# Attention scores q·kᵀ: input loads issued behind a head's third copy instead of its second

## The chip, the cores and the metric

The kernel runs on one core of a Trainium2 chip. The time is device time in microseconds (us) for one launch. The runs before the change gave a median of 1063.17 us (three runs, 1063.16 to 1063.77).

The core's engines have short names here: PE does matmuls (PEld is its weight loads), DVE, ACT and POOL are the vector, scalar and general engines, SP issues transfers. Each has its own queue of instructions, which it works through in order. A transfer (DMA) is issued by an instruction on SP's or ACT's queue and then carried out by 16 DMA engines, which all transfers share.

## The reference

```python
def setup_inputs():
    batch, n_heads, seq, head_dim = 8, 12, 1024, 64
    # q, k: (8, 12, 1024, 64) float32, normal, times 0.1

def reference(q, k):
    return np.einsum('bhid,bhjd->bhij', q, k).astype(np.float32)
```

For each of 96 heads (8 x 12), a 1024 x 64 matrix q is multiplied with the transpose of a 1024 x 64 matrix k. The inputs are 50.3 MB together, the result is 402.7 MB: a head's result alone is 4 MB.

## The kernel before

**Blocks.** The 96 heads are cut into 11 blocks of 2, 2, 4, 8, 8 and then six times 12 heads (line 33), numbered 0 to 10 here. A block's q and k are each loaded with one transfer (`Block.load`, line 66; the DMA is line 73), except in blocks 0 and 1, which are loaded head by head (line 84). A load of a 12-head block is 3072 KB, of an 8-head block 2048 KB. Blocks 0 to 2 are loaded at once into a tile that is later used for results ("early"). The others go into tiles of a pool with two places (`in_pool`, tag "x", the tile is `x_sb`), so a load has to wait until the content of two loads before has been cast.

**From load to matmul.** POOL casts a loaded tile to 16 bit in pieces (line 127, `cast_quads`), into a pool of five `half_sb` tiles. DVE transposes each piece in 32 x 32 squares (line 145, `transpose_quads`) into the block's `qT` and `kT`, of which there are two sets: one for the block being computed, one for the next. Blocks 0 and 1 go another way, through PE (line 151).

**A head.** `scores` (line 156) computes one head. With w = 2, which holds for all but the first head, it runs four steps, u = 0 to 3. In each, PE does four matmuls into one of two PSUM tiles `ps` (line 171), and ACT copies that tile, 128 x 2048 numbers, into the head's result tile `o_sb` (line 181). There are three result tiles. After a step, `scores` calls whatever the dictionary `side` holds for that u. Behind the fourth copy, SP issues the head's result as one transfer of 4096 KB (line 185). A head can only begin to copy when the result of three heads before has been written out.

**Where the next loads are issued.** `block` (line 238) calls `scores` for each head of a block and fills `side`: under 0 the transposes for the next block, and, in two heads of each block, under 1 a call of `next_load`, which takes the next (block, q or k) from the list `stream` and issues its load on ACT's queue. Which heads these are stands in `LOADS` (line 263): heads 1 and 3 of block 2, heads 4 and 6 of blocks 3 and 4, heads 6 and 8 of the later ones. What is loaded during block i belongs to block i + 2. The first two loads into `x_sb`, block 3's, are issued before all heads (line 217), one on SP's queue and one on ACT's.

**Order.** Every instruction is given to `keep_in_program_order` (`pin`), so each engine's queue runs in the order in which the code is written. After a head, `to_half` (line 225) puts the casts of what has been given a load by then into POOL's queue, up to block i + 2.

Of the kernel before, what the change touches and what calls it, by code (L numbers as in the profile page):

```python
# [13 lines left out]
def kernel(  # L14
# [6 lines left out]
    nc = tc.nc  # L21
# [190 lines left out]
    def next_load(eng):  # L212
        if stream:
            b, x = stream.pop(0)
            b.load(x, eng)
# [9 lines left out]
    def to_half(last):  # L225
        while casts:
            i, c = casts[0]
            if i > last or (blocks[i], c[0]) in stream:
                return
            blocks[i].cast_quads(*c)  # L230
            casts.pop(0)
# [6 lines left out]
    def block(i, heads, ps_pool, w):  # L238
        b = blocks[i]
        nxt = blocks[i + 1] if i + 1 < len(blocks) else None  # L240
        for n in heads:
            side = {}
            if nxt and nxt.by_pe:
                if n == 1:
                    side = {
                        u: [
                            lambda x=u // 2: nxt.transpose_rows(
                                x, ps_pool, nc.vector.tensor_copy
                            )
                        ]  # L250
                        for u in (1, 3)
                    }
            elif nxt:
                parts = nxt.chunks()
                some = [s for m, s in enumerate(parts) if m * b.N // len(parts) == n]
                side = {0: [lambda s=s: nxt.transpose_quads(*s) for s in some]}

            if n in LOADS.get(i, (6, 8)):
                side[1] = side.get(1, []) + [lambda: next_load(nc.scalar)]
            b.scores(n, side, ps_pool, w)  # L260
            to_half(i + 2 + (n == b.N - 1))

# [4 lines left out]
    with tc.tile_pool(name="first_pool", bufs=4, space=bass.MemoryType.PSUM) as pool:  # L267
        for x in range(2):
            blocks[0].transpose_rows(x, pool, (nc.vector.tensor_copy, nc.scalar.copy)[x])
        block(0, [0], pool, 1)  # L270
    po_pool = ctx.enter_context(
        tc.tile_pool(name="po_pool", bufs=2, space=bass.MemoryType.PSUM)
    )
    block(0, [1], po_pool, 2)
    for i in range(1, len(blocks)):
        if i + 1 < len(blocks):
            blocks[i + 1].alloc()
        block(i, range(blocks[i].N), po_pool, 2)
# [30 lines left out]
```

## Time and profile before

| what | value |
|---|---|
| median of the runs | 1063.17 us |
| profiled execution, span | 1061.2 us |
| PE busy | 701.0 us (66%) |
| ACT busy | 697.3 us (66%) |
| DVE busy | 471.3 us (44%) |
| POOL busy | 368.3 us (35%) |
| moved by DMA | 453.25 MB, mean 427 GB/s |
| result transfers | 96 of 4096 KB, median 21.8 us from issue to landing |
| loads of 12-head blocks | 12 of 3072 KB, median 22.2 us (q) and 21.9 us (k) |

The profile is of one execution; its span is the time from its first to its last instruction, and the runs' time is taken around it. A group of instructions is named by line, engine and operation, with the tile it writes and the tile it reads (`o_sb<-ps`). "Idle" is time in which the engine stood still just before that group, and behind the arrow stands what ended most of it. ACTq and SPq are the queues of ACT and SP at work, issuing a transfer for example. The DMA share is the mean busy share of the 16 DMA engines.

ACT's idle time and PE's hang together: PE waits for ACT to empty a PSUM tile (325.5 us in total, 188 times), and ACT waits for a result tile to be written out.

### The profile page before, as it was taken

The numbers are of one execution on the slowest core, as the hardware profiler recorded it, in microseconds if no ns is written. First come the engines' busy times: TensorE is split into PE (matmuls) and PEld (weight loads), VectorE is DVE, ScalarE is ACT, GpSimd is POOL, SyncE is SP. The second block draws the span as 40 slices with busy tenths as digits, with TensorE's granted clock in tenths as the row PEclk, the third lists the DMA queues.
The fourth block names the chain that finished last, engine by engine and source line by source line (L and its number), as shares of the span: only waits on it lengthen the run. The fifth ranks groups of instructions, "written<-read, shape, count | busy, mean of one in ns | idle before, by whom it ended". The sixth has DMA issues, their size and how long they took to land.

```text
span 1061.2 us, 4282 instructions
## 1 busy us (share of the span) xinstructions
PE 701.0 (66%) x1568; PEld 241.5 (23%) x1568; DVE 471.3 (44%) x75; ACT 697.3 (66%) x386; POOL 368.3 (35%) x286
## 2 busy tenths in 40 slices
PE   6866755765677557775577855777557777778770
PEld 2322211221222112221122211222112222222220
DVE  2999502990795007960079600795007950000000
ACT  4866755755677556775577755777557777777771
POOL 6967228607720463304633046320463200000000
DMA  9999999999999999999999999999999999999997
GB/s 375 434 435 434 434 432 429 432 430 429 429 434 431 429 438 429 435 422 428 434 434 433 425 424 437 432 431 426 432 430 434 434 434 430 430 435 430 433 431 319
DMA packets 17588, 453.25 MB, mean 427 GB/s; under 512 B 1952, under 2 KB 1952, under 8 KB 2976
## 3 DMA queue, kind: packets, MB, share of 16 engines
q1 hardware_dynamic: 14688, 406.85, 89.2%
q10 hardware_dynamic: 2880, 46.14, 10.3%
q8 instruction: 12, 0.20, 0.1%
q14 instruction: 8, 0.07, 0.0%
HBM read 50.33 MB, written 402.65 MB: 427 GB/s over the span
## 4 chain that ended last, share of the span: by engine, by line
DMA 71%; ACT 18%; PE 8%; issue 1%; DVE 0%; POOL 0%; ACTq 0%; SPq 0%
DMA out_dram<-o_sb 71%; ACT o_sb L181 18%; PE ps L171 8%; DMA early<-in_q_dram 0%; PE ps L151 0%; POOL half_sb L97 0%; ACTq L181 0%; DVE kT L154 0%; DVE o_sb L179 0%; ACT kT L154 0%; SPq L84 0%
## 5 line engine op out<-in xcount | busy, mean ns | idle before, releaser
L181 ACT COPY o_sb<-ps 128x2048 f32<-128x2048 f32 (+1 forms) x384 | 695.0, 1860 | 334.6 <-DMA out_dram<-o_sb 306.2
L171 PE MATMUL ps<-kT,qT 64*128 64x512 f16 x1536 | 696.9, 617 | 329.2 <-ACT o_sb L181 325.5
L127 POOL CAST half_sb<-x_sb 32x1536 f16<-32x1536 f32 (+1 forms) x256 | 346.5, 1353 | 454.5 <-DMA x_sb<-in_q_dram 315.0
L171 PEld LDWEIGHTS <-qT 64*128 64x128 f16 x1536 | 238.3, 157 | 786.0 <-issue 781.3
L145 DVE STREAM_TRANSPOSE qT<-half_sb 128x1536 f16<-128x1536 f16 (+1 forms) x34 | 232.7, 7140 | 372.0 <-issue 314.9
L145 DVE STREAM_TRANSPOSE kT<-half_sb 128x1536 f16<-128x1536 f16 (+1 forms) x34 | 234.3, 7198 | 0.0
L127 POOL CAST half_sb<-early 32x1024 f16<-32x1024 f32 x16 | 16.5, 1034 | 3.9 <-DMA early<-in_q_dram 3.2
L151 PE MATMUL ps<-ident,half_sb 128*128 128x128 f16 x32 | 4.1, 308 | 6.6 <-POOL half_sb L97 6.0
L154 DVE COPY qT<-ps 128x1024 f16<-128x1024 f16 x2 | 2.5, 1225 | 12.1 <-PE ps L151 12.1
L179 DVE COPY o_sb<-ps 128x1024 f32<-128x1024 f32 x4 | 4.9, 1224 | 4.3 <-PE ps L171 4.3
L97 POOL CAST half_sb<-early 128x512 f16<-128x512 f32 x8 | 4.6, 613 | 4.1 <-DMA early<-in_q_dram 4.1
L151 PEld LDWEIGHTS <-half_sb 128*128 128x128 f16 x32 | 3.2, 139 | 8.4 <-POOL half_sb L97 6.3
L154 ACT ACT_TABLE_LOAD x1 | 1.3, 1283 | 5.6 <-DMA early<-in_q_dram 5.6
L154 DVE COPY kT<-ps 128x1024 f16<-128x1024 f16 x1 | 1.2, 1225 | 4.3 <-PE ps L151 4.3
L154 ACT COPY kT<-ps 128x1024 f16<-128x1024 f16 x1 | 1.0, 1012 | 1.2 <-PE ps L151 1.2
masks.py:199 POOL TENSOR_SCALAR_AFFINE_SELECT ident<-ident 128x128 f16<-128x128 f16 x1 | 0.3, 292 | 0.1
masks.py:197 POOL MEMSET ident<- 128x128 f16 x1 | 0.2, 204 | 0.3 <-POOLq L293 0.3
L293 POOL MEMSET const-float32-0.0<- 128x1 f32 x1 | 0.1, 98 | 0.2 <-issue 0.2
L293 POOL MEMSET const-bfloat16-1.0<- 128x1 bf16 x1 | 0.1, 100 | 0.0
L293 POOL MEMSET const-uint8-127<- 128x1 uint8 x1 | 0.1, 100 | 0.0
L293 POOL MEMSET const-float32-1.0<- 128x1 f32 x1 | 0.1, 98 | 0.0
## 6 DMA issues: line engine op xcount, KB each, us to landing
out_dram<-o_sb SPq DMA_DIRECT2D x96, 4096.0 KB, 21.8
x_sb<-in_q_dram ACTq DMA_DIRECT2D x6, 3072.0 KB, 22.2
x_sb<-in_k_dram ACTq DMA_DIRECT2D x6, 3072.0 KB, 21.9
x_sb<-in_k_dram ACTq DMA_DIRECT2D x2, 2048.0 KB, 19.0
x_sb<-in_q_dram SPq DMA_DIRECT2D x1, 2048.0 KB, 18.2
x_sb<-in_q_dram ACTq DMA_DIRECT2D x1, 2048.0 KB, 18.5
early<-in_k_dram ACTq DMA_DIRECT2D x4, 256.0 KB, 5.0
early<-in_q_dram SPq DMA_DIRECT2D x4, 256.0 KB, 4.7
```

The source lines that it names most:

```text
L97: nc.gpsimd.tensor_copy(out=self.rows[x][:, :, half], in_=self.raw[x][:, half * n : (half + 1) * n].rearrange("p (r d) -> p r d", d=D),)
L127: nc.gpsimd.tensor_copy(out=half_sb[q0 : q0 + 32].rearrange("p (r d) -> p r d", d=32), in_=raw[32 * b : 32 * b + 32, c * m : (c + 1) * m, h],)
L145: pin(nc.vector.transpose(out=dst, in_=src))
L151: pin(nc.tensor.transpose(t_ps[:, t], self.rows[x][:, t], ident))
L154: pin(copy(out=dst, in_=src))
L171: nc.tensor.matmul(ps[:, at : at + 512], qT[cs, g, w * u + tt], kT[cs, g, js],)
L179: pin(nc.vector.tensor_copy(out=dst, in_=ps))
L181: pin(nc.scalar.copy(out=dst, in_=ps))
L293: nc = _bacc.Bacc("TRN2", target_bir_lowering=False, num_devices=1)
```

## The change

One line of `block`: the call of `next_load` goes into `side` under 2 instead of 1, so it is made behind the third of a head's four steps.

```diff
             if n in LOADS.get(i, (6, 8)):
-                side[1] = side.get(1, []) + [lambda: next_load(nc.scalar)]
+                side[2] = side.get(2, []) + [lambda: next_load(nc.scalar)]
             b.scores(n, side, ps_pool, w)
```

On ACT's queue each of these 14 loads changes places with one copy (line 181). The queues of SP, PE, DVE and POOL hold the same instructions in the same order as before, and the order in which transfers are issued is the same.

## The prediction

> **What bounds the kernel now.** I read the page's slices and queues first, then the chain of work that ended last, then the waits, and last the stretches in which a load runs beside the results.
>
> ```profile
> DMA  9999999999999999999999999999999999999997
> q1 hardware_dynamic: 14688, 406.85, 89.2%
> q10 hardware_dynamic: 2880, 46.14, 10.3%
> DMA 71%; ACT 18%; PE 8%; issue 1%; DVE 0%; POOL 0%; ACTq 0%; SPq 0%
> L181 ACT COPY o_sb<-ps 128x2048 f32<-128x2048 f32 (+1 forms) x384 | 695.0, 1860 | 334.6 <-DMA out_dram<-o_sb 306.2
> ```
>
> The two queues that carry data (q1, with nearly all its bytes from SP, and q10, with ACT's loads) keep the 16 DMA engines busy for 89.2 + 10.3 = 99.5% of the span. That is 1055.9 of 1061.2 us. The chain is mostly result transfers. ACT, the busiest compute engine beside PE, sits idle for 334.6 us, 306.2 of them until a result has landed and freed an output tile. So compute waits for the DMA engines. To be sure that this holds where the edit acts, I cut the span into stages (the columns after the length are busy time of each engine, the clock, the DMA share and GB/s):
>
> ```profile
> 0.00:20.00 20.00, 11.53 (x38) 5.12 (x39) 6.12 (x5) 6.82 (x7) 11.75 (x21) 1.00 0.94 376
> 20.00:60.00 40.00, 35.80 (x91) 12.83 (x90) 33.14 (x9) 34.09 (x20) 38.00 (x37) 1.00 1.01 425
> 60.00:200.00 140.00, 86.86 (x192) 29.69 (x192) 82.96 (x17) 86.88 (x49) 79.13 (x65) 1.00 1.00 432
> 200.00:840.00 640.00, 420.35 (x927) 143.92 (x926) 325.09 (x43) 420.94 (x233) 239.45 (x164) 1.00 1.00 431
> ```
>
> From 20 us on the DMA share is 1.00 (1.01 comes from packets counted at a stage's edge). The loads that the edit moves are issued at 56.1 us (the first) to 759.9 us (the last), all inside these stages.
>
> Now one such load, and a stretch without one (ACT's timeline; start, length, what, and in brackets the idle time before it):
>
> ```profile
> 469.28 1.86 ACT L181 COPY o_sb<-ps 128x2048 f32<-128x2048 f32 x1 [2.34 <-DMA out_dram<-o_sb]
> 469.33 0.33 ACTq L73 DMA_DIRECT2D x_sb<-in_q_dram  x1
> 471.04 1.87 ACT L181 COPY o_sb<-ps 128x2048 f32<-128x2048 f32 x1
> 473.09 3.64 ACT L181 COPY o_sb<-ps 128x2048 f32<-128x2048 f32 x2 [0.18 <-PE ps L171]
> 483.52 3.64 ACT L181 COPY o_sb<-ps 128x2048 f32<-128x2048 f32 x2 [6.79 <-DMA out_dram<-o_sb]
> ...
> 522.88 3.63 ACT L181 COPY o_sb<-ps 128x2048 f32<-128x2048 f32 x2 [5.09 <-DMA out_dram<-o_sb]
> ...
> 933.48 3.63 ACT L181 COPY o_sb<-ps 128x2048 f32<-128x2048 f32 x2 [2.32 <-DMA out_dram<-o_sb]
> ...
> 943.25 3.63 ACT L181 COPY o_sb<-ps 128x2048 f32<-128x2048 f32 x2 [2.33 <-DMA out_dram<-o_sb]
> ```
>
> The load sits behind the head's second copy in the code, yet its issue stands at 469.33, 0.05 us into the first copy: ACT's queue hands its copies on and runs ahead as long as the next one's data are there. Without loads a head takes 943.25 - 933.48 = 9.77 us. The four heads from 469.28 to 522.88, with a q and a k load among them, take 53.60 us, so the two loads cost 53.60 - 4 x 9.77 = 14.52 us. Their 2 x 3072 KB are 6.29 MB, and at the 432 GB/s of the table's third row that makes 14.56 us. A load costs its bytes, and no more.
>
> **The change, part by part.** Nothing is added or removed. 14 load issues on ACT (those in the head loop; the first two stand before it) move behind one more copy. The order of SP's, PE's, DVE's and POOL's work and the order of the DMAs among themselves stay.
>
> *The issue.* The third copy is handed on when PE has filled its tile, at 473.09 in the rows above. The load's issue should then stand at about 473.1 to 473.2 instead of 469.33: 3.8 us later (only 2 us in the head at 54 us, where the copies already wait for PE). What it now delays on ACT is the fourth copy, which lies behind the third: 1.8 us of copying cover the 0.33 us of issuing. Were this cover gone, 14 x 0.33 = 4.7 us of ACT work would be exposed. But ACT waits 2.3 us or more before each head for a landed result, so it would shorten that wait. Value taken: 0.
>
> *The wait before the issue.* A load waits until POOL has cast the input tile's previous content. The four semaphore waits recorded on the load's line took 0.017 us each. Later too there is room: block 6's k load, issued at 250.93, takes the tile of block 5's k, whose last cast ended at 201.61 + 5.97 = 207.6. A later issue only widens that gap. Cost 0, and no new wait stands before the fourth copy.
>
> *The DMA engines.* What I must exclude is that they run dry for want of the load. When ACT starts a head, the result of three heads ago has just landed and the two between are still to be written: 2 x 9.77 = 19.5 us of work. The head's own result is issued 7.5 us later (copies from 469.28 to 476.73). So 12 us of work are left at the worst moment, without any load. A load that comes 3.8 us later fits in three times. In the head at 54 us the third result before landed at 66.2, where ACT's idle time ends, so the queue is as full there. Idle time added: 0.
>
> *Who waits for the load.* POOL casts it, DVE transposes the casts, and the next block's matmuls read them. The tightest place is block 5:
>
> ```profile
> 208.82 31.16 DVE L145 STREAM_TRANSPOSE kT<-half_sb 128x1536 f16<-128x1536 f16 x4
> 271.32 1.86 PE L171 MATMUL ps<-kT,qT 64*128 64x512 f16 x4 [0.19 <-ACT o_sb L181]
> ```
>
> Its last transpose ends at 240.0 and its first matmul starts at 271.32: 31.3 us to spare, against a load that lands some 4 us later. Block 4's ends at 102.33 + 18.88 = 121.2 for a start at 178.34. From block 6 on, DVE waits 70 us and more for the transposed tiles to come free. Cost 0.
>
> *Mixing reads and writes.* This is the one cost that the trace can't exclude. Today a load starts where one result has just landed; then it will start 3.8 us into the next one's 9.77. The stretches with a pair of loads (469.3 to 522.9, 601.2 to 655.0, 733.1 to 786.7) show 426, 426 and 427 GB/s, those without (877 to 931, 931 to 985) 431 and 433. A loss of 432 - 426 = 6 over 432, times 53.7 us and 7 pairs, makes 5.2 us in the whole run, though the head starts above show none. Bounds: -5.2 us if the shift removed the loss, +5.2 if it doubled it. I take 0: the same packets meet the same number of others, shifted by 40% of a result. As the head starts see no loss at all, I keep a third of the bounds (1.7 us) for the likely case.
>
> [...] The trace first: loads take a median of 22.2 and 21.9 us from issue to landing, while their bytes are worth 7.3 us of all engines. [...]
>
> *Sum.* 1061.2 us of span + 0 for the issue, 0 for the waits, 0 for the engines, 0 for the mixing = 1061.2. The median of the runs, 1063.17, lies 2.0 us above the span, which the edit doesn't touch. Forecast 1063.2.
>
> **The rivals.** *A, faster: the loss from mixing goes.* Up to 5.2 us, so 1058.0 to 1061.0. For it: the 426 against 432 GB/s. Against it: the head starts, which charge a pair of loads no more than its bytes.
>
> *B, slower: the load meets the results at a worse phase.* Place: the two or three results written while a load is under way, 7 times a pair. Price: the loss of 5.2 us doubled, 1068.4; it decides by over 0.2% once these stretches fall from 426 to below 423.5 GB/s (2.1 us / (7 x 53.7 us) = 0.56%). For it: the q load's own stretch, 469.3 to 496.0, shows 419 GB/s and the k load's, 496.0 to 523.0, shows 433, so the place of a load in time may matter. Against it: such short stretches count packets at their edges.
>
> *C, slower: the load comes too late for block 5.* It needs 31.3 us of delay before PE waits, and then 12 more before the DMA engines do; 10 us beyond that would give 1073. The delay is 3.8 us, so I give it next to nothing.
>
> *D, the change hardly does what it says:* ACT's queue runs so far ahead that the issue moves by less than 1 us. Against it: the third copy's tile isn't filled before 473.09. It would give 1063.2 too.
>
> **How the numbers follow.** About 0.2%, 2.1 us, is what a measurement of this kernel can tell from no change. Forecast with D: 0.87 (D 0.03 of it), from 1062.0 to 1065.0, which is the third of the mixing bounds either way, a little less below since the head starts leave nothing to win. A: 0.05. B: 0.07, C: 0.01. Faster 0.05, the same 0.87, slower 0.08. The range 1062.0 to 1065.0 leaves out A and nearly all of B and C, 0.13 together.
>
> **What would show it.** In the profile after: load issues about 0.1 us after the start of a third copy; ACT's idle times in the heads around a load shared out otherwise (6.8, 5.1, 6.8, 5.1 us before the four heads that follow a q load now), with the same sum, so that the four heads still take 53.6 us; casts starting 2 to 4 us later; q1 and q10 at 99.5% again; no PE wait for a transpose beyond those of the first block. I am wrong if the DMA share between 60 and 840 us falls below 1.00, if the pair stretches leave 426 GB/s by more than 2, or if PE waits for DVE in block 5.

## The result, and the profile after

The changed kernel takes 1067.24 us, the median of seven runs (1064.28 to 1069.84), against 1063.22 us before (seven runs, 1063.15 to 1063.77). The ratio is 1.0033, with a 95% interval of 1.0024 to 1.0042: slower by 4 us, and spread over 5.6 us where the kernel before was spread over 0.6. (A ratio is taken over all the runs, not from the two medians.) In another set of runs the same kernel took 1065.73 us (1.0040, 1.0023 to 1.0056). The forecast was no change, 1062.0 to 1065.0 us.

The profiled execution took 1067.25 us, with a span of 1065.5 us, 4.2 more than before (1065.47 against 1061.24). The rows that bounded the kernel before look nearly the same on the page after:

```profile
DMA  9999999999999999999999999999999999999996
q1 hardware_dynamic: 14688, 406.85, 88.9%
q10 hardware_dynamic: 2880, 46.14, 10.3%
DMA 71%; ACT 17%; PE 9%; issue 1%; DVE 0%; POOL 0%; ACTq 0%; SPq 0%
L181 ACT COPY o_sb<-ps 128x2048 f32<-128x2048 f32 (+1 forms) x384 | 695.1, 1860 | 338.3 <-DMA out_dram<-o_sb 308.0
```

The two data queues are busy for 99.2% of 1065.5 us. The page rounds its shares; the times of the packets themselves (a packet is one record of what an engine moved; a result is 128 of them, of 32 KB and a median of 1.213 us) add up to 1056.7 us as a mean over the 16 engines, against 1055.9 us before. So only 0.8 of the 4.2 us is more work. The other 3.4 us are engines standing idle, nearly all of it at the very end. The stages of the last 20 us, first before and then after (after the length: busy time of each compute engine, clock, DMA share, GB/s):

```profile
1041.20:1051.20 10.00, 0.00 (x0) 0.00 (x0) 0.00 (x0) 0.00 (x0) 0.00 (x0) 1.00 1.04 449
1051.20:1061.20 10.00, 0.00 (x0) 0.00 (x0) 0.00 (x0) 0.00 (x0) 0.00 (x0) 1.00 0.28 121
```

```profile
1045.50:1055.50 10.00, 0.00 (x0) 0.00 (x0) 0.00 (x0) 0.00 (x0) 0.00 (x0) 1.00 0.91 390
1055.50:1065.50 10.00, 0.00 (x0) 0.00 (x0) 0.00 (x0) 0.00 (x0) 0.00 (x0) 1.00 0.11 46
```

Nothing computes here; the last results are being written. After the change, the share in the last 10 us is 0.11, about 2 of 16 engines at work, and 0.91 in the 10 us before. The other engines have finished and wait for a few. A share that reads 1.00 all along the kernel is a mean, and doesn't show who is behind.

The trace holds the answer in another place: every transfer leaves 16 completion marks (1952 for 122 transfers), which I take as one from each DMA engine. I call "lag" how far the last engine's mark of a transfer stands behind the middle of the 16. For the last result of the run, the marks around their middle, in us:

```
before  last mark at 1060.3 us
  -0.9 -0.8 -0.5 -0.5 -0.5 -0.5 -0.3 -0.3  0.3  0.5  0.6  1.7  1.8  2.6  3.0  5.9
after   last mark at 1064.5 us
  -0.1 -0.1  0.0  0.0  0.0  0.0  0.0  0.0  0.0  0.3  0.8  0.9  1.3  2.9  8.9  9.4
```

The middle engine ends at 1054.4 us before and at 1055.1 after, 0.7 us later. The last engine's lag grows from 5.9 to 9.4 us, by 3.5. Together that is the 4.2 us between the two last marks. The lag at the first of each pair of loads shows when it grew:

```
lag of the result that landed last ahead of each pair's first load, and at the end, us
before   1.5  1.6  1.5  2.8  3.5  3.6  4.0   end 5.9
after    1.6  2.5  3.3  3.7  4.4  6.5  7.7   end 9.4
```

ACT's timeline shows it too, since a head can start only when the last engine has written an old result. The last pair of loads, before and after:

```profile
733.09 1.86 ACT L181 COPY o_sb<-ps 128x2048 f32<-128x2048 f32 x1 [2.31 <-DMA out_dram<-o_sb]
733.14 0.33 ACTq L73 DMA_DIRECT2D x_sb<-in_q_dram  x1
...
747.37 3.63 ACT L181 COPY o_sb<-ps 128x2048 f32<-128x2048 f32 x2 [6.82 <-DMA out_dram<-o_sb]
...
786.74 3.64 ACT L181 COPY o_sb<-ps 128x2048 f32<-128x2048 f32 x2 [5.07 <-DMA out_dram<-o_sb]
```

```profile
736.59 3.64 ACT L181 COPY o_sb<-ps 128x2048 f32<-128x2048 f32 x2 [2.32 <-DMA out_dram<-o_sb]
740.40 1.87 ACT L181 COPY o_sb<-ps 128x2048 f32<-128x2048 f32 x1 [0.18 <-PE ps L171]
740.41 0.33 ACTq L73 DMA_DIRECT2D x_sb<-in_q_dram  x1
...
765.57 3.64 ACT L181 COPY o_sb<-ps 128x2048 f32<-128x2048 f32 x2 [9.98 <-DMA out_dram<-o_sb]
...
793.31 3.65 ACT L181 COPY o_sb<-ps 128x2048 f32<-128x2048 f32 x2 [8.67 <-DMA out_dram<-o_sb]
...
928.85 3.63 ACT L181 COPY o_sb<-ps 128x2048 f32<-128x2048 f32 x2 [2.24 <-DMA out_dram<-o_sb]
...
938.52 1.87 ACT L181 COPY o_sb<-ps 128x2048 f32<-128x2048 f32 x1 [2.22 <-DMA out_dram<-o_sb]
```

The load's issue stands 3.82 us behind the head's start (740.41 against 736.59). ACT's longest wait in these rows grows from 6.8 to 10.0 us, and the four heads take 793.31 - 736.59 = 56.7 us, where they took 786.74 - 733.09 = 53.65. In blocks 5, 6 and 7 the same four heads take 0.9, 1.6 and 0.6 us more than before. Some of it comes back without loads: a head then takes 938.52 - 928.85 = 9.67 us, against 9.77 before.

### The profile page after: what moved, and what is told of

It is laid out like the page before. It is cut to its first block, busy times and chain, and to the rows that moved or that the text cites. A ratio compares the mean times of both kernels' runs of the same rounds, so it can differ in the third digit from the quotient of the medians.

```text
span 1065.5 us, 4282 instructions
## 1 busy us (share of the span) xinstructions
PE 701.1 (66%) x1568; PEld 241.3 (23%) x1568; DVE 471.5 (44%) x75; ACT 697.4 (65%) x386; POOL 369.1 (35%) x286
## 2 busy tenths in 40 slices
DMA packets 17588, 453.25 MB, mean 425 GB/s; under 512 B 1952, under 2 KB 1952, under 8 KB 2976
## 3 DMA queue, kind: packets, MB, share of 16 engines
q10 hardware_dynamic: 2880, 46.14, 10.3%
## 4 chain that ended last, share of the span: by engine, by line
DMA 71%; ACT 17%; PE 9%; issue 1%; DVE 0%; POOL 0%; ACTq 0%; SPq 0%
DMA out_dram<-o_sb 71%; ACT o_sb L181 17%; PE ps L171 8%; DMA early<-in_q_dram 0%; PE ps L151 0%; POOL half_sb L97 0%; DVE kT L154 0%; DVE o_sb L179 0%; ACTq L181 0%; ACT kT L154 0%; SPq L84 0%
## 6 DMA issues: line engine op xcount, KB each, us to landing
out_dram<-o_sb SPq DMA_DIRECT2D x96, 4096.0 KB, 21.8
x_sb<-in_q_dram ACTq DMA_DIRECT2D x6, 3072.0 KB, 22.3
```

## The experiments

"Lag" below is that of the profiled execution's last result. Differences are against the kernel before on the same chip and in the same set of runs, where its median was 1063.05 to 1063.22 us. The sets ran on different chips: one had the change again, the first and the fourth copy, SP's queue, k alone, the half loads and the 15 engines; a second the halves, the result held back with the change, the long wait and no loads; a third its control, the two shorter waits and q alone. So runs are best compared with the kernel before, and less surely with each other. The diffs show the lines that matter, against the kernel before.

| run | load's issue after the head's start, us | median, us | against before | middle engine's end, us | lag, us |
|---|---|---|---|---|---|
| the kernel before | 0.05 | 1063.22 | | 1054.4 | 5.9 |
| first copy | 0.02 | 1063.14 | 0.0 | 1055.3 | 4.5 |
| short wait | 0.4 | 1063.42 | +0.4 | 1055.0 | 4.9 |
| longer wait | 1.1 | 1064.10 | +1.0 | 1056.5 | 4.0 |
| long wait | 2.7 to 3.9 | 1064.46 | +1.4 | 1054.3 | 7.3 |
| the change | 3.8 | 1067.24 | +4.0 | 1055.1 | 9.4 |
| the change again | 3.8 | 1065.73 | +2.6 | 1055.3 | 6.9 |
| q alone | 3.8 (q), 0.05 (k) | 1066.62 | +3.6 | 1055.4 | 7.8 |
| k alone | 0.05 (q), 3.8 (k) | 1064.14 | +1.0 | 1055.7 | 5.8 |
| fourth copy | 5.6 | 1064.79 | +1.7 | 1054.2 | 7.1 |

The three waits act on 10 of the 14 loads (the times are of these); in the kernel before, the first head's load stands at 1.8 us, the others at 0.05 to 0.1. The last two columns are of one execution each. The first copy's differ from the kernel before's by 0.9 and 1.4 us at the same time, so differences of that size in them say little.

**The change again.** No edit.

> The changed kernel again, for the spread of its times and to see whether the same happens in another execution. Theory PHASE (a load whose packets begin in the middle of a result's makes one of the 16 DMA engines lag, and the last engine sets the end): median 1065 to 1069 us and runs some 2 to 6 us apart, with the last results landing late because one engine ends 5 us or more behind the middle of the 16. Theory CHANCE (the 1067 us came from disturbed runs): 1063 to 1064 us.

Ten runs lay between 1064.96 and 1073.57 us, with a median of 1065.73. The slowdown is there again, with its spread; two runs lie above 1071. The profiled one was the fastest of the ten and still has a lag of 6.9 us, with three more engines between 5.4 and 6.2. CHANCE falls.

**Behind the first copy.**

```diff
-                side[1] = side.get(1, []) + [lambda: next_load(nc.scalar)]
+                side[0] = side.get(0, []) + [lambda: next_load(nc.scalar)]
```

> The load is issued behind the first copy of the head instead of the second. ACT's queue ran ahead before, so the issue should stand at the first copy's start in any case, where it also stood before. PHASE: no change against the kernel before, 1063 to 1064 us. A theory that goes by the place in the code (COPIES: each copy further costs) says 1060 to 1063 us.

1063.14 us (ratio 1.0001, 0.9993 to 1.0010), with the issue 0.02 us after the head's start (0.05 before). So it isn't the place in the code by itself that costs; the time of the issue is what changed.

**Behind the fourth copy.** `side[3]` in the same line.

> The load is issued behind the fourth copy, some 5.6 us after the head's start and 1.8 us before SP issues the head's result. PHASE (the middle of a result is bad, 5.6 of 9.8 us is as far in as 3.8): 1065 to 1069 us. [...] Theory LATE (later is worse, through what waits for the load): 1068 us and more, with PE waiting for DVE.

1064.79 us, 1.0016 (1.0008 to 1.0025), just below what PHASE gave. LATE falls: later, it costs less than the change. Nor is it the nearness to SP's next issue, 1.8 us ahead here and 3.7 in the changed kernel. The loss is not a matter of the load being late.

**On SP's queue.**

```diff
-                side[1] = side.get(1, []) + [lambda: next_load(nc.scalar)]
+                side[1] = side.get(1, []) + [lambda: next_load(nc.sync)]
```

> The 14 loads are issued on SP's queue between two results, in the same heads, so results and loads pass each engine one behind the other and are not mixed. PHASE and any theory in which mixing two queues makes packets longer: packets keep their usual length, the engines stay together, 1059 to 1062 us. [...] Theory READ (a load costs its extra because it reads while results write, however ordered): 1063 us as before.

1066.33 us, 1.0030 (1.0018 to 1.0042), all five runs within 1.1 us. The load goes out right behind the previous head's result:

```profile
468.96 0.33 SPq L185 DMA_DIRECT2D out_dram<-o_sb  x1
469.38 1.12 SPq L73 DMA_DIRECT2D x_sb<-in_q_dram  x1
```

PHASE's 1059 to 1062 us and READ's 1063 were missed. That the load stands only 0.42 us from a result's issue would fit the loss, but the fourth copy had spoken against such nearness. Packets didn't get longer in sum: results' packets ran over their usual 1.213 us by 1.1 us (mean of the 16 engines), against 2.8 before, the loads' packets over theirs by 3.8 us, against 2.1, and all packets took 1055.9 us in both. And yet the lag is 9.4 us, since it grows by 0.1 us a result all through the load-free end (7.1 at 848 us to 9.4 at 1063 us) and no load stretch takes anything back. One engine falls behind the others steadily.

**The result in halves.** In the 14 heads with a load, and in the same four heads of blocks 9 and 10, which have none, SP sends the result as two transfers, behind the second and the fourth copy; the loads stay.

```diff
+                if halves and u % 2:
+                    store(NT // 2 * (u // 2), NT // 2)
```

> Loads where the kernel before has them, but in the 14 heads with a load the result goes out as two transfers of 2 MB, the first issued behind the second copy, some 3.7 us after the load: the distance that the changed kernel has between its load and the result's issue. [...] Theory PHASE (only what the engines are writing when the load's packets come matters): 1063 to 1064 us.

1070.51 us, 1.0073 (1.0061 to 1.0085): beyond PHASE's 1063 to 1064 and the changed kernel's time, with a lag of 10.4 us. It speaks for the 3.7 us from the load's issue to a result's as the cause, but halving the results also halves their packets (20181 packets carry the run's 453.26 MB, where 17588 carried 453.25 before). Where there is no load, that costs nothing: in blocks 9 and 10 the four heads from the first halved one on take 39.0 us, against 39.1 before. What smaller packets cost beside a load is not shown.

**The result held back, with the change.** In 10 of the 14 heads with a load (blocks 3 and 5 to 8) a DVE copy of half the result onto itself stands before the result's issue.

```diff
+            if late:
+                end = o_sb[:, NT // 2 :].rearrange("p t j -> p (t j)")
+                pin(nc.vector.tensor_copy(out=end, in_=end))
```

> [...] PHASE: as the changed kernel, 1065 to 1069 us, with the last engine's lag growing at every pair of loads.

**The same without the change** (loads behind the second copy), as its control.

> The control for the run with the result's issue held back: loads behind the second copy as before, the result's issue held back by the same DVE copy in 10 of 14 heads. If the loss there came from the loads' place (PHASE, SELECT): 1063 to 1064.5 us here. If holding a result back starves the engines that are ahead: as slow here, 1066 us or more, with idle engines between 200 and 1055 us.

With the change 1069.99 us (1.0064, 1.0043 to 1.0085), without it 1063.46 us (1.0004, 0.9995 to 1.0013). (The same heads of blocks 9 and 10, which have no load, hold their results back too.) The result is issued 6.0 us behind the load in the one and 9.7 to 11.0 us in the other. In the changed kernel that distance is 3.7 us, and a load's first packet starts 3.5 to 4.5 us behind its issue, at about the time of the result's issue. With 6.0 us the loss isn't gone, so the two meeting there doesn't explain it in this form. Holding a result back costs next to nothing by itself, but it makes the load's place dearer, 6.5 us instead of 2.6 to 4.0. In the run with the change, the packet records between 200 and 1055 us show 3.3 us without work, as a mean of the 16 engines, where the kernel before has 0.002 and the changed kernel 0.3. The lag there reached 18.8 us (at 798 us). By the prediction's sum a result is issued with some 12 us of older results left, counted on the last engine; an engine further ahead of it than that would have nothing left and stand. At the end the lag is 7.4 us, and the middle engine itself ends 7.6 us later than in the kernel before: in this run the loss is not the lag of one engine.

**Waits of 0.4, 1.1 and 2.7 us before the load.** The loads stay behind the second copy, but in 10 of 14 heads the load's tile is first written by DVE, which waits for the head's result tile (0.4 and 1.1 us: two DVE writes, of 300 or 1000 numbers) or for the first copy (2.7 us in six heads, 2.9 to 3.9 in four: a DVE copy of 1000 numbers).

```diff
+            if hold is not None:
+                pin(nc.vector.memset(o_sb[:, 0, :1], 0.0))
+                pin(nc.vector.memset(hold[:, :300], 0.0))
```

> Loads behind the second copy, but in 10 of 14 heads they wait for two small DVE writes that begin when the head's result tile comes free: issue some 0.4 to 0.7 us after the head's start instead of 0.05, about half of one packet of 1.213 us. SELECT as a matter of packets (the load spares the last engine because it comes at a fixed point of that engine's packet): part of the loss shows already, 1064 us or more, and the last engine loses more than 3 us in the load stretches. PHASE (depth into the result): 1063 to 1063.6 us.

> The same with a longer DVE write: issue some 0.8 to 1.4 us after the head's start, about a whole packet. SELECT by packets: back near the time before, 1063 to 1063.7 us, less than with the half packet. PHASE: between the time before and the 1064.5 us at 2.7 us, so 1063.3 to 1064 us.

> Loads behind the second copy, as before, but in 10 of 14 heads the load also waits for a DVE copy that itself waits for the head's first copy: issue some 3.1 us after the head's start, against 0.05 before and 3.8 in the changed kernel, and 4.3 us ahead of the result's issue. PHASE, growing with depth into the result: 1065 to 1067 us. [...] Theory SELECT (a load disturbs the last engine unless it starts right when that engine has finished a result): 1065 us or more, like every other place but the first.

1063.42 (1.0002, 0.9994 to 1.0011), 1064.10 (1.0009, 1.0001 to 1.0018) and 1064.46 us (1.0012, 1.0004 to 1.0021). The issue of the first stands here, 0.42 us into the head's first copy:

```profile
469.00 0.06 DVE L169 MEMSET o_sb<- 128x1 f32 x1 [31.45 <-DMA out_dram<-o_sb]
469.14 1.87 ACT L188 COPY o_sb<-ps 128x2048 f32<-128x2048 f32 x1 [2.62 <-DVE o_sb L169]
469.16 0.31 DVE L170 MEMSET x_sb<- 128x300 f32 x1
...
469.56 0.34 ACTq L77 DMA_DIRECT2D x_sb<-in_q_dram  x1
```

The loss rises with the issue's distance from the landing, without the up and down that SELECT by packets wanted: 0.0, 0.4, 1.0, 1.4 us at 0.02, 0.4, 1.1, 2.7 us, the 0.4 not clear of no change. The rise fits PHASE, its size doesn't: the long wait's 1064.46 us is below PHASE's 1065 to 1067 and SELECT's 1065. At 1.1 us the loss isn't the lag: there it is 4.0 us, and the middle engine itself ends late, at 1056.5 us.

**No loads in the head loop.** Blocks 4 to 10 use block 3's inputs.

> All 14 loads of the head loop are left out, and blocks 4 to 10 use block 3's inputs (its tiles are filled up with 2 MB more at the start), so the results of these blocks are those of other inputs. Bytes: 14 loads are 41.9 MB less, 2.1 MB more, at 432 GB/s 92.2 us less. If loads at the place before cost their bytes alone: 970 to 972 us. If they cost the last engine extra even there (up to the 5.2 us of the bound): 966 to 970 us. The last engine's lag at the end then shows what results alone bring: 0.1 us a result, some 5 to 9 us.

971.34 us, 91.7 us below the kernel before, for 39.8 MB less (92.2 us at 432 GB/s). So at the place before, the loads cost their bytes and nothing else. The last 10 us of this run:

```profile
949.60:959.60 10.00, 0.00 (x0) 0.00 (x0) 0.00 (x0) 0.00 (x0) 0.00 (x0) 1.00 1.00 429
959.60:969.60 10.00, 0.00 (x0) 0.00 (x0) 0.00 (x0) 0.00 (x0) 0.00 (x0) 1.00 0.14 60
```

The lag is 6.8 us, the second engine's only 1.5: without any load, one engine falls behind steadily (1.1 us at 126 us, 3.9 at 362, 5.1 at 597, 6.4 at 832). The kernel before, at 5.9, stands no worse for its 14 loads. The changed kernel, at 9.4, does.

**The change for q alone, and for k alone.**

```diff
-                side[1] = side.get(1, []) + [lambda: next_load(nc.scalar)]
+                u = 1 + (n == LOADS.get(i, (6, 8))[0])
+                side[u] = side.get(u, []) + [lambda: next_load(nc.scalar)]
```

(with `!=` instead of `==` for k)

> The change for the 7 q loads alone; the k loads stay behind the second copy. If each load's place adds by itself: about half of the changed kernel's 2.5 to 4 us, 1064.2 to 1065.2 us. If q's or k's place alone matters: 1063 to 1063.5 or 1065.5 to 1067 us.

> The counterpart of the run with q alone: the k loads behind the third copy, the q loads behind the second. If each load's place adds by itself: the rest of the changed kernel's loss, 1064 to 1065 us. If the first load of a pair sets which engine pays (q alone gave 1066.6 us): 1063 to 1063.8 us.

q alone 1066.62 us (1.0030, 1.0019 to 1.0041), k alone 1064.14 us (1.0009, 1.0000 to 1.0018). The first load of a pair carries most of it: q alone costs 3.6 us, as much as both together (2.6 to 4.0). But k alone isn't free: its 1.0 us (the edge of what its interval can tell from nothing) is above the 1063 to 1063.8 us expected if only the first load set which engine pays.

**Half loads, in both places.** The loads bring half of each partition's row.

```diff
+                m = self.elems // 2
+                pin(nc.gpsimd.memset(to[:, m:], 0.0))
+                to, of_ = to[:, :m], of_[:, :m]
```

> The 14 loads bring only the first half of each partition's row, the other half is set to zero by POOL, so blocks 4 to 10 are computed from half of their inputs. Loads behind the second copy. 21.0 MB less at 432 GB/s are 48.5 us less: 1014 to 1015 us. The base for the next run.

> The same half loads behind the third copy. If what the last engine loses comes with each load's arrival (theory ARRIVAL): 2.5 to 4 us above the run before, as with whole loads. If it comes with the time in which load and results share the engines (theory SHARE): half of that, 1.2 to 2 us above it.

1015.96 and 1017.29 us: 1.3 us apart, as SHARE had it. With four runs each (1015.41 to 1016.14 and 1016.37 to 1018.67) this leans to SHARE and doesn't settle it. The base missed its own forecast of 1014 to 1015 us: half loads at the old place save 1.4 us less than their bytes.

**The last result on 15 engines.**

```diff
+            cuts = [0, P] if self.first + n < BH - 1 else [0, 120, P]
```

> The kernel before, but the very last result is written as two transfers, of 120 and of 8 partitions. [...]

Were one engine left out of the larger transfer, and were it the one that ends last, the end should have come earlier. It took 1070.21 us, 7 us more. The transfer of 120 partitions took 28.9 us from issue to landing, where whole results take 21.8. Of its 16 marks one stands 0.5 us behind the issue, the other 15 between 1053.9 and 1067.8 us, which fits 15 engines with eight packets each. What took the time was longer packets: of the results' packets that start after 1038.5 us, 82 of 207 took over 1.5 us, in the kernel before none of 208, and together they took 22.3 us instead of 15.8 (mean of the 16 engines). Why splitting this transfer made packets longer is not shown, and the trace doesn't name the engines, so which one lags stays open. No version was found that beats the kernel before.

## Why the prediction was wrong

The bound (the DMA engines), the new issue time (3.8 us later; 2.4 in the first head, forecast 2), the wait before the issue and the consumers were right. One row was misread: the result that landed at 66.2 us frees the head that starts at 66.28, not the one at 54 us, for which it landed at 54.17. Nothing hangs on it, since two results were still to be written there too. Block 5's last transpose ends at 208.06 + 31.19 = 239.3 us, for a first matmul at 270.93. What the load's lateness would cost, rival C, was rightly nothing; the run with the loads on the fourth copy, later still, costs less than the change.

**The step that failed** is "Mixing reads and writes", taken at 0 with a third of its bounds, 1.7 us, as the likely case. It measured 4.0 us, and 2.6 us in the second set. Two things were wrong in it.

First, the argument. "The same packets meet the same number of others" is nearly true of the mean: 0.8 us more packet time. But the end is set by the last engine, not by the mean, and its lag grew by 3.5 us. The prediction counted the 16 engines as one resource, in the DMA share of 1.00 and in "idle time added: 0" alike. The unequal marks were in the trace before: a lag of 5.9 us at the end, and of 1.5 us already at 56 us.

Second, the evidence. "The head starts above show none" was true of the old place only. That place isn't just any point: the head starts when the last engine has finished a result, and the load was issued 0.05 us later. I strung the packet records to 16 rows, each packet to the one that ends where it begins, and summed up by how much packets ran over their usual length in the 30 us behind the 14 loads:

```
                      the engine that finished last   mean of the other 15
before                            1.0                        3.0
the change                        7.0                        3.6
the change again                  4.6                        4.2
q alone                           6.9                        4.2
fourth copy                       2.6                        3.1
first copy                        3.1                        3.4
result held back, change          14.5                       5.8
result held back, control         1.8                        4.0
```

In us; the records don't name the engine, so the rows are inferred, and another rule for stringing gives other numbers in nearly the same order (2.3 for the kernel before, 9.4 for the change). In most of these versions the others lose about the same, 3 to 4 us, and the last engine loses least in the kernel before and most in the slowest versions. This suggests that most of the loss is in who pays, not in how much is paid. It doesn't show it. The first copy (3.1, no slower than before) and the fourth (2.6, slower by 1.7 us) stand in the wrong order. And k alone, slower by only 1.0 us, comes to 8.0 where the change has 9.4, all of it in the 30 us behind the q loads, which were not moved. ACT's timeline agrees: there the head behind the last q load waits 7.67 us, against 6.82 before.

```profile
734.79 0.33 ACTq L73 DMA_DIRECT2D x_sb<-in_q_dram  x1
...
749.86 3.64 ACT L181 COPY o_sb<-ps 128x2048 f32<-128x2048 f32 x2 [7.67 <-DMA out_dram<-o_sb]
```

**Rival B** had the place (the results written while a load is under way) and nearly the price (1068.4). Its mechanism, a fall of the rate in these stretches below 423.5 GB/s, didn't happen: the same three stretches show 426, 425 and 424 GB/s after, and the changed kernel's own four heads with a pair of loads 428, 429 and 427. So its number came near by luck. It was given 0.07, on the same mean-only argument. The test by the four heads' 53.6 us, on the other hand, was a good one, and it failed as said: 54.5 to 56.7 us after.

**What stays open.** That moving the issue from the landing to 3.8 us after it costs 2.6 to 4.0 us, is shown, and that in the profiled execution 3.5 of 4.2 us are the last engine's lag. It is not so everywhere: the lag's part of the later end is 1.0 of 1.9 us in the change again and 1.9 of 2.9 with q alone; with the longer wait and k alone the lag is smaller than before and the middle engine is late. Why the last engine often pays when the load comes some us after its landing is not shown: this cause stays open. Nor is it shown why 5.6 us costs less than 3.8, why q's load matters more than k's, and why a result in halves costs 7 us.

## What to carry to other kernels

Where transfers bound a kernel and their share reads 1.00, look at the spread of the engines' completion marks: the end is the middle engine's end plus the last one's lag (here 1054.4 + 5.9 us before, 1055.1 + 9.4 after). The load issued 0.05 us after a landing was tied to the DMA engine that finished last, and moving the issue by 3.8 us untied it. Here that cost time though the mean share stayed at 1.00; that it would elsewhere is not shown. The effect was 0.3%, with run-to-run spread nine times that of the kernel before, so a single pair of runs says little.

## What the runs showed of the hardware that was not expected

In the run without loads, one of the 16 DMA engines (taken to be the same one throughout) fell behind by 0.05 to 0.12 us for each 4096 KB result: from 1.1 to 3.9 us over the 24 results from 126 to 362 us, from 5.1 to 6.4 over those from 597 to 832 us, 6.8 us after 96 results. A head without a load took 9.77 us in the kernel before, where the lag grew (4.4 us at 845 us, 5.9 at the end), and 9.67 us in the changed kernel, where the lag of the last engine, perhaps another one, was shrinking (10.3 us at 850 us, 9.4 at the end). ACT's queue ran a load's issue ahead of the end of two copies that stand before it (469.33 us, with the copies running to 472.91), so moving it from the second copy to the first changed nothing (1063.14 us, against 1063.22).
